# A decoder trunk on eight cores: one channel group instead of two follows the token tiles, the second becomes a plain slot with the last tiles between, the norm row comes in four row strips, and one P buffer set remains

## The chip, the cores and the metric

The kernel runs on all 8 cores of one Trainium2 chip, which are two dies of four cores each. The time of an execution is the time of the slowest core in microseconds (us) on the device. A kernel's time is the median of several executions.

Some executions fall in a slower state: one die shows a lower granted clock than the other (0.81 to 0.98 on the one, 0.98 to 0.99 on the other) and the time is 1.6% to 17.7% above the fastest of the same kernel in the same rounds. Those executions are marked slow; they are not compared with anything. All profiles that are read below are of fast executions. TensorE's clock has two levels in these traces, a granted share of 1.00 and one of 0.50; "full rate" and "half rate" below mean these two.

A core's trace is read against a set of marks (start of the first projection, start of the first full convolution, and so on), and where I say "median of the cores" I mean that I read the mark on each of the eight cores of one profiled execution and took the median.

## The reference, cut to what matters

One layer of a hybrid decoder trunk, run on a batch of prompts and on a batch of short samples:

```python
def layer(x, ...):
    m = mixer(rms_norm(x, g_mix_pre), ...)
    x = x + rms_norm(m, g_mix_post)
    f = conv_ffn(rms_norm(x, g_ffn_pre), ...)      # up-projection, conv(3), gelu gate, down-projection
    return x + rms_norm(f, g_ffn_post)

def mixer(xn, ...):
    a_val, a_gate, b_x, b_gate = split(xn @ w_in)
    u  = a_val * sigmoid(a_gate)                    # group A: 8 channel groups of 128
    ca = silu(layer_norm(causal_dwconv(u, 31 taps)))
    xc = causal_dwconv(b_x, 4 taps)                 # group B: 8 heads of 128
    h  = rglru(xc, ...)                             # a scan along the tokens
    cb = h * gelu(b_gate)
    return concat(ca, cb) @ w_out
```

Everything that the change touches lies in the first 410 us, in `rms_norm`, the projections with `w_in`, and the convolution of group A. Each core has 17 tiles of 128 tokens. A tile is loaded, squared and scaled by its norm, transposed on TensorE, and copied from PSUM (`ps` in the profiles, which the matmuls write) to SBUF (`sb_...`, which they read). The projections of this kernel read that copy and wait for it.

## The kernel before: the parts that the change and the argument touch

A tile is normed on ScalarE (square, logarithm, exponential) and VectorE (one multiply with the gain row), and turned on TensorE:

```python
def p0_norm(n):
    ...
    act(xs, xt, AF.Square, ..., accum=c[:, 0:1])           # ScalarE, reads the loaded tile
    act(c[:, 1:2], c[:, 0:1], AF.Ln, ...)
    act(c[:, 2:3], c[:, 1:2], AF.Exp, ...)
    stt(xs, xt, c[:, 2:3], T["grow0"], mult, mult, ...)    # VectorE, 2.35 us
    if n + XD(n) < 17: p0_load(n + XD(n))

def p0_turn(n):
    # 16 transposes of 128x128 into two PSUM banks (6 and 7),
    # then copies PSUM -> xna (and xnp) on VectorE and ScalarE
    ...
```

The first channel groups follow the tiles as they come. In the kernel before these are two groups (j = 0 and 1), so per pair of tiles TensorE has two gate and value projections and two pieces of convolution:

```python
load_w(4, after=[("xt0",)])                 # four 1 MB weights first
p0_load(1)
for n in range(2, 5):
    p0_load(n, [(f"wu{n - 1}",)])           # tile 2 waits for weight 1, and so on
...
for g in range(5):
    for j in range(2):
        if g > 0 and j == 0:
            p0_norm(2 * g + 2)
            p0_norm(2 * g + 3)
        ...
        early(g, j)                         # gate and value projection of this piece of tokens
        if g >= 2:
            early_conv(g - 2, [j])          # 31 taps as matmuls with diagonal matrices
        if g > 0:
            p0_turn(2 * g + 2 + j)
```

After the last tile, seven rounds of the same kind follow: gate and value projections of one channel group, the convolution of that group, and a P block of group B (its `b_x` projection, gates and scan). I call this the steady stretch. The P blocks work on the tokens in `xnp`. The next stage, the Q stage, runs group B over the tokens in `xna` (projections `X` and `b`, gelu, gates, scan) and the LayerNorm of group A. The turn into it reads:

```python
bx7 = triple(); P_bx(7, bx7)                # last P projection, into a group of three PSUM banks
...
QX, QB = 3, 0
proj(QX, "X", 0, ACT3)                      # next projection, into the same three banks
...
proj(QB, "b", 0, CAT3, g0=30)
P_gate(7, "wab"); P_sig(7, "p1", V_BA)      # sigmoid
bs = ln_sum("A3b", QX); act(T["mu"], ...)
P_gate(7, "wxb"); P_sig(7, "p3", V_BX)      # sigmoid
Q_gelu(0, QB); done_w("b", 0)               # gelu: a table load of 1.28 us ahead of it
bq = ln_sum("A3", QB)                       # TensorE, needs the banks QB that gelu reads
```

All buffers have fixed places in SBUF, from a table of offsets. A buffer may lie over another whose life has ended. The first write to it then waits for the last reader of the old one.

## Time and profile before

The median of three executions is 1850.44 us (1849.97 to 1850.83).

| | before |
|---|---|
| span of the slowest core in the profile | 1849.0 us |
| TensorE busy | 95% of it |
| first projection, median of the cores | 20.9 us |
| twelfth tile (n = 11 in the code) turned | 105.1 us |
| first full convolution starts | 140.6 us |
| last P projection ends | 373.1 us |
| second X projection starts (Q stage under way) | 404.7 us |
| up-projection starts | 702.0 us |

The first line of the page that I use is the busy table. It gives for each engine the busy time in us, its share of the span and the number of instructions:

```profile
PE 1764.0 (95%) x10470; PEld 918.3 (50%) x10470; DVE 989.7 (54%) x998; ACT 569.1 (31%) x1016; POOL 131.6 (7%) x248
```

PE is TensorE, DVE is VectorE and ACT is ScalarE. TensorE bounds the kernel. Which stretch of time could be saved does not stand in this line, so here are the windows of the same core (core 3). Each line is one stretch: its limits, its length, the busy time of each engine with its instruction count, the mean clock that TensorE was granted (1.00 is full rate, half rate counts as 0.50), and the share of the DMA engines in use with the GB/s:

```profile
20.00:40.00 20.00, 9.78 (x96) 8.74 (x96) 10.75 (x12) 8.35 (x16) 0.00 (x0) 0.80 1.02 287
40.00:60.00 20.00, 17.79 (x156) 14.63 (x157) 13.40 (x11) 14.68 (x27) 1.06 (x2) 0.86 0.79 256
60.00:80.00 20.00, 19.50 (x170) 15.01 (x169) 10.19 (x9) 9.14 (x17) 0.00 (x0) 1.00 0.54 144
80.00:100.00 20.00, 19.50 (x203) 17.54 (x201) 9.72 (x12) 10.67 (x20) 1.06 (x2) 1.00 0.27 52
100.00:120.00 20.00, 17.73 (x169) 12.78 (x167) 10.77 (x11) 9.35 (x17) 1.06 (x2) 1.00 1.03 243
120.00:140.00 20.00, 16.06 (x160) 12.12 (x158) 13.65 (x11) 10.42 (x14) 2.64 (x5) 0.86 0.72 129
```

TensorE is idle for 10.2 us from 20 to 40 us. It is almost full from 60 to 100 us at full rate, and it loses again from 100 to 140 us, partly at a reduced clock. The view of TensorE's waits (line, what it waited for, us in total, times, longest) for 20 to 410 us says which waits those are (four of its lines):

```profile
PE ps L473 <- DVE sb_xs_107 L372: 6.2, 1, 6.2
PE ps L473 <- DVE sb_xnp_138 L351: 6.2, 3, 3.9
PE ps L378 <- ACT sb_gbg_95 L345: 3.9, 1, 3.9
PE ps L378 <- ACT sb_bxpZ L343: 2.2, 1, 2.2
```

L473 is the transpose, L378 the matmul. The 6.2 us are the wait for tile 2, which was loaded late behind a weight. The 3.9 us to `sb_xnp` lie at the last tiles. The wait for `sb_gbg` is the late gelu, and the wait for `sb_bxpZ` is the evacuation of the last P projection: these two are the turn. The timeline of TensorE around 77 us shows the loop at its best. The columns are start, length, engine, line, operation, number of instructions, and in brackets the idle time ahead with what ended it:

```profile
74.20 1.03 PE L378 MATMUL ps<-sb_xna_137,sb_wu_192 128*128 128x256 bf16 x8 [0.50 <-DVE sb_xna_137 L351]
...
90.43 1.03 PE L378 MATMUL ps<-sb_xna_137,sb_wu_192 128*128 128x256 bf16 x8 [0.50 <-DVE sb_xna_137 L351]
```

The same projection (the first weight of a piece) comes back after 90.43 - 74.20 = 16.2 us, with only 0.5 us of idle time ahead. So a pair of tiles costs 16.2 us here, and matmul work fills it.

### The profile page before, as it was taken

The numbers are of one execution on the slowest core, as the hardware profiler recorded it, in microseconds if no ns is written. First come the engines' busy times: TensorE is split into PE (matmuls) and PEld (weight loads), VectorE is DVE, ScalarE is ACT, GpSimd is POOL, SyncE is SP. The second block draws the span as 40 slices with busy tenths as digits, with TensorE's granted clock in tenths as the row PEclk, the third lists the DMA queues.
The fourth block names the chain that finished last, engine by engine and source line by source line (L and its number), as shares of the span: only waits on it lengthen the run. The fifth ranks groups of instructions, "written<-read, shape, count | busy, mean of one in ns | idle before, by whom it ended". The sixth has DMA issues, their size and how long they took to land.

```text
span 1849.0 us, 33818 instructions; the slowest of 8 cores (1840.2 to 1849.0 us)
## 1 busy us (share of the span) xinstructions
PE 1764.0 (95%) x10470; PEld 918.3 (50%) x10470; DVE 989.7 (54%) x998; ACT 569.1 (31%) x1016; POOL 131.6 (7%) x248
## 2 busy tenths in 40 slices
PE   5989999989987999999999999999999999999996
PEld 3765555644443444555555544444555555544442
DVE  4564565458885564666666640001666666663245
ACT  4552442358882443222222211111222212211111
POOL 0010000001120001000000000001000000000000
PEclk8999999999998999999999999999999999999998
DMA  9482243212268438644333335556444433359556
GB/s 248 127 182 38 47 84 53 37 35 49 44 115 221 166 137 182 115 69 69 66 67 66 68 68 120 120 120 120 70 69 70 69 66 67 67 136 250 103 159 217
DMA packets 55318, 193.22 MB, mean 104 GB/s; under 512 B 7393, under 2 KB 11361, under 8 KB 48993
## 3 DMA queue, kind: packets, MB, share of 16 engines
q0 software_dynamic: 30144, 110.34, 34.8%
q1 hardware_dynamic: 24994, 80.71, 13.0%
q8 instruction: 84, 1.38, 0.3%
q14 instruction: 96, 0.79, 0.2%
HBM read 266.52 MB, written 32.35 MB: 162 GB/s over the span
## 4 chain that ended last, share of the span: by engine, by line
PE 91%; DMA 3%; ACT 3%; issue 2%; DVE 1%; DVEq 0%; POOL 0%; ACTq 0%; SPq 0%; POOLq 0%
PE ps L378 90%; DMA sb_wo_213<-w_out 1%; PE ps L473 1%; DMA sb_wu_193<-w_in 1%; DMA sb_xt_106<-xall 1%; ACT L345 0%; PE ps L1159 0%; DMA sb_xt_96<-xall 0%; DVE sb_ht L372 0%; ACT sb_xs_1_132 L347 0%; ACT sb_t_1_128 L345 0%; ACT sb_t_0_114 L345 0%; DVE sb_xna_137 L351 0%; DVE sb_xs_102 L372 0%; DVE sb_xs_107 L372 0%
## 5 line engine op out<-in xcount | busy, mean ns | idle before, releaser
L351 DVE COPY sb_ve_120<-ps 128x1026 f32<-128x1026 f32 (+1 forms) x48 | 36.4, 801 | 297.4 <-PE ps L378 294.9
L351 DVE COPY sb_ve_134<-ps 128x1026 f32<-128x1026 f32 (+1 forms) x48 | 36.4, 801 | 114.0 <-PE ps L378 114.0
L372 DVE SCALAR_TENSOR_TENSOR sb_og_135<-sb_ge_133,sb_vecs,sb_og_135 128x1184 f32<-128x1184 f32 x48 | 69.7, 1452 | 5.7 <-DVE sb_og_135 L372 0.9
L372 DVE SCALAR_TENSOR_TENSOR sb_ov_136<-sb_ve_134,sb_vecs,sb_ov_136 128x1184 f32<-128x1184 f32 x48 | 69.7, 1452 | 5.0
L372 DVE SCALAR_TENSOR_TENSOR sb_ov_122<-sb_ve_120,sb_vecs,sb_ov_122 128x1184 f32<-128x1184 f32 x48 | 69.7, 1451 | 5.0
L372 DVE SCALAR_TENSOR_TENSOR sb_og_121<-sb_ge_119,sb_vecs,sb_og_121 128x1184 f32<-128x1184 f32 x48 | 69.7, 1451 | 5.0
L343 ACT COPY sb_dstg<-ps 128x512 f32<-128x512 f32 x36 | 20.9, 587 | 159.5 <-PE ps L378 159.5
L378 PE MATMUL ps<-sb_ubf_124,sb_diag_123 128*128 128x342 bf16 (+3 forms) x527 | 63.9, 284 | 1.2 <-DVE sb_ubf_124 L363 1.2
L378 PE MATMUL ps<-sb_ubf_110,sb_diag_109 128*128 128x342 bf16 (+3 forms) x527 | 62.3, 279 | 0.7 <-ACT sb_ca_199 L345 0.7
L343 ACT COPY sb_ffo<-sb_ve_134 128x32 f32<-128x32 f32 x24 | 5.3, 219 | 182.1 <-DVE sb_ve_134 L351 182.1
L343 ACT COPY sb_ffo<-sb_ve_120 128x32 f32<-128x32 f32 x24 | 5.3, 219 | 175.5 <-DVE sb_ve_120 L351 175.5
L345 ACT ACT_TABLE_LOAD x38 | 48.8, 1283 | 31.6 <-PE ps L378 19.6
L378 PEld LDWEIGHTS ps<-sb_ubf_124,sb_diag_123 128*128 128x128 bf16 x527 | 46.6, 100 | 18.4 <-issue 1.6
L345 ACT ACTIVATE sb_og_135<-sb_og_135 128x1184 f32<-128x1184 f32 x24 | 28.6, 1191 | 84.0 <-DVE sb_og_135 L372 84.0
L378 PEld LDWEIGHTS ps<-sb_ubf_110,sb_diag_109 128*128 128x128 bf16 x527 | 44.9, 97 | 17.6 <-issue 0.9
L345 ACT ACTIVATE sb_og_121<-sb_og_121 128x1184 f32<-128x1184 f32 x24 | 28.6, 1190 | 79.6 <-DVE sb_og_121 L372 79.6
L343 ACT COPY sb_ge_119<-ps 128x1026 f32<-128x1026 f32 (+1 forms) x48 | 31.4, 707 | 32.9 <-PE ps L378 32.9
L343 ACT COPY sb_ge_133<-ps 128x1026 f32<-128x1026 f32 (+1 forms) x48 | 31.4, 706 | 27.4 <-PE ps L378 27.4
L378 PE MATMUL ps<-sb_xn_139,sb_wp_214 128*128 128x512 bf16 (+1 forms) x192 | 35.2, 325 | 0.5 <-DVE sb_xn_139 L351 0.5
L378 PE MATMUL ps<-sb_xn_139,sb_wp_216 128*128 128x512 bf16 (+1 forms) x192 | 35.1, 325 | 0.3 <-ACT sb_ge_119 L343 0.3
L378 PE MATMUL ps<-sb_xn_142,sb_wp_214 128*128 128x512 bf16 (+1 forms) x192 | 35.1, 325 | 0.1
L378 PE MATMUL ps<-sb_xn_139,sb_wp_225 128*128 128x512 bf16 (+1 forms) x192 | 35.2, 325 | 0.0
(736 smaller groups left out, 4084.9 us busy)
## 6 DMA issues: line engine op xcount, KB each, us to landing
f_scr<-sb_dstg SPq DMA_DIRECT2D x36, 256.0 KB, 3.5
sb_xt_96<-xall SPq DMA_DIRECT2D x5, 1024.0 KB, 11.0
sb_x_0_117<-xall SPq DMA_DIRECT2D x5, 1024.0 KB, 5.0
h_scr<-sb_x_0_117 SPq DMA_DIRECT2D x5, 1024.0 KB, 5.4
sb_xt_101<-xall SPq DMA_DIRECT2D x4, 1024.0 KB, 12.3
sb_xt_106<-xall SPq DMA_DIRECT2D x4, 1024.0 KB, 11.0
sb_x_1_131<-xall SPq DMA_DIRECT2D x4, 1024.0 KB, 4.9
sb_wp_214<-w_up POOLq DMA_DIRECT2D x8, 512.0 KB, 6.2
```

Of the source, the lines that this page charges most:

```text
L343: S.op("act", lambda e: e.copy(out=out, in_=in_), reads, writes)
L345: S.op("act", lambda e: e.activation(out=out, in_=in_, func=func, scale=scale, bias=bias), reads, writes)
L351: S.op("dve", lambda e: e.tensor_copy(out, in_), reads, writes)
L372: S.op("dve", lambda e: e.scalar_tensor_tensor(out, a, s, b, op0, op1), reads, writes)
L378: S.op("pe", lambda e: e.matmul(out, lhsT, rhs, start=start, stop=stop, skip_group_check=skip), reads, writes)
L473: S.op("pe", lambda e, pb=pb, j=j, k=k: e.transpose(pb[:, 128 * j:128 * j + 128], xs[:, 128 * k:128 * k + 128], identb[:]), [ks, "identb"] ...
```

## The change

Its intent is to get through the tiles sooner. With one channel group following, a pair of tiles costs TensorE less, two weights are enough to start with, and the last tiles are turned between the thirds of the second group's projections, where TensorE has other work. The norm row is loaded in four pieces to partitions 0, 32, 64 and 96, so that four small matmuls with one row each can spread it. The Y set of P buffers goes, and the loop over the groups becomes uniform. At the turn, the counter of the PSUM bank groups skips one (`trip["n"] += 1`), so that the next projection does not need the banks that are still being evacuated, and gelu runs ahead of the two sigmoids. All buffers get new places.

The core of the diff (cut: the table of places, lifetimes, `vecs` loaded ahead of tile 0, the building of the conv diagonals in two parts, and the rewritten inner order of the steady stretch):

```diff
-        seq += [("g", 0), ("v", 0), ("g", 1), ("v", 1), ("g", 2), ("v", 2), ("x", 0), ("x", 1), ("g", 3), ("v", 3), ("x", 2)]
-        for j in range(4, 8):
+        seq += [("g", 0), ("v", 0), ("g", 1), ("v", 1), ("x", 0)]
+        for j in range(2, 8):
 ...
-        load("sp", r_su, T["grow0"][0:1, :], grows_d[0:1, :], [], ...)
+        for c in range(4):
+            load("act", r_ga, T["grow0"][32 * c:32 * c + 1, 512 * c:512 * c + 512], grows_d[0:1, 512 * c:512 * c + 512], [], ...)
 ...
-        load_w(4, after=[("xt0",)])
+        load_w(2, after=[("xt0",)])
         p0_load(1)
         for n in range(2, 5):
-            p0_load(n, [(f"wu{n - 1}",)])
+            p0_load(n, [("wu0",)])
 ...
-        for g in range(5):
-            for j in range(2):
-                ... early(g, j); early_conv(g - 2, [j]); p0_turn(2 * g + 2 + j)
+        for g in range(1, 5):
+            early(g)
+            p0_turn(2 * g + 2)
+            p0_norm(2 * g + 4)
+            if g >= 2:
+                early_conv(g - 2)
+            p0_turn(2 * g + 3)
+            p0_norm(2 * g + 5)
 ...
+        p0_turn(12); p0_norm(14)
+        proj(bg, "g", 1, ACT3, only=0)
+        early_conv(3); done_w("v", 0)
+        p0_turn(13); p0_norm(15)
+        proj(bg, "g", 1, ACT3, only=1)
+        ...
+            if j == 7:
+                trip["n"] += 1
 ...
         proj(QB, "b", 0, CAT3, g0=30)
+        Q_gelu(0, QB)
+        done_w("b", 0)
         P_gate(7, "wab")
-        P_sig(7, "p1", V_BA)
         bs = ln_sum("A3b", QX)
         ...
+        P_sig(7, "p1", V_BA)
+        bq = ln_sum("A3", QB)
         P_gate(7, "wxb")
         P_sig(7, "p3", V_BX)
-        Q_gelu(0, QB)
```

## The prediction

> **What bounds the kernel now.** By the page's busy table TensorE is busy 95% of 1849 us. The 20 us windows place its idle time: about 32 us before 200 us, 1.4 us from there to 370, some 29 us from 370 to 600, little later. The change keeps the matmul work, so only idle times and half-rate stretches can move.
>
> *Start.* In the waits and the timeline, TensorE waits 3.0, 3.5 and 4.9 us for the first two tiles and 6.2 us for tile 2, which landed only at 31.0 us: its load waits for the second of four 1 MB weights (20.1 us), then took 10.8 us. From 54 to 106 us TensorE has almost no gap: with two channel groups, 16.2 us of work per pair of tiles. From 106 to 144 us it loses 1.9, 3.9 and 0.7 us around the last tiles, plus half rate after: 16 transposes take 1.87 us instead of 1.06, 62 conv matmuls 5.26 instead of 3.64. [...]
>
> *Turn into the Q stage.* At 376.7 us TensorE waits 2.2 us for the evacuation of the last P block (same PSUM triple as the next projection), at 399 and 400 us 0.7 and 3.9 us (gelu queued behind two sigmoids and a 1.28 us table load). Two half-rate stretches add about 3.4 us.
>
> **What changes.**
> 1. Norm row in four row strips [...] instead of 7.2 us in series: worth 0.3 us, as the row's last copy ends at 11.0 us and the first norm could start at 10.8. Vecs ahead of tile 0 costs about 0.7.
> 2. Two weights instead of four ahead of tiles 2 to 4: tile 2 lands near 22 us.
> 3. Per pair of tiles TensorE has 9.2 us (3.5 gate and value, 2.1 transposes, 3.6 conv). But evacuation, square and norm (1.0+2.7 us ScalarE, 2.35 VectorE) stand between the two transposes, then a 1.3 us evacuation: about 11.5 us per pair. So the loop turns from matmul-bound to chain-bound, with gaps of 1 to 6 us. I expect the eleventh tile turned near 80 us instead of 106, with 27.4 us less work done: the early arrival is mostly given back.
> 4. The last tiles lie between the thirds of the second group's projections: one or two gaps of 2 us, no half rate. At the start of its conv (near 108 us; the old kernel reaches the same state at 144 less 31 us) about 4 us are gained.
> 5. One P buffer set: about 1.3 us lost at j=2, as much as the old gaps at 189 and 229 us. Neutral.
> 6. The skipped triple and the earlier gelu remove the 2.2 and most of the 4.6 us. But VectorE's chain into the Q stage does not move, and ScalarE is nearly full from 425 us: about 4.5 us.
>
> **Prediction.** 1850.4 - 4.3 - 4.5 = about 1841 us, 8 times in 10 within 1830 to 1851. Faster by over 2%: 0.01; within 2%: 0.97; slower: 0.02.
>
> **Signs.** Right: tile 2 lands by 24 us; TensorE's idle in 50 to 106 us rises to over 8 us, waiting for VectorE's copies of xna; no half-rate stretch in 106 to 144; no 2.2 and 3.9 us waits near 377 and 400; same length from 600 us on. Wrong: tile loads waited for after 40 us, or the loop at full rate.
>
> **What would make it wrong.** Half rate through the sparser loop; weights colliding with tiles 7 to 9; the new placement making a load of w_out or w_up wait; ScalarE in the Q stage eating the gain.

## The result, and the profile after

| | before | after |
|---|---|---|
| median | 1850.2 us of 4 | 1889.88 us of 4 |
| all executions | 1849.97, 1850.44, 1850.83, 1849.01 | 1848.32, 2089.98 (slow), 1846.8, 1931.45 (slow) |
| ratio of fast executions | | 0.9986 (95% interval 0.9962 to 1.0011) |

A ratio here is the mean time of one kernel's fast runs over that of the other's of the same rounds, so it is not quite the ratio of the medians quoted. Two of the four executions of the changed kernel fell in the slow state, and they pull its median to 1889.88 us, outside the predicted range. That says nothing of the change: in later rounds the kernel before also had such executions, for instance 2106.47 and 2139.37 us. The two fast executions lie inside the range. But the gain is 2 or 3 us, not the 9.4 us (1850.4 - 1841) that I had summed up. This section and the experiments are about where the rest went.

The busy table tells nothing of it:

```profile
PE 1765.4 (96%) x10375; PEld 910.2 (49%) x10375; DVE 988.6 (54%) x994; ACT 564.2 (31%) x1000; POOL 131.6 (7%) x248
```

It misleads here: the busy time hardly moved (1764.0 and 1765.4 us), since matmuls at half rate count as busy for longer (32 of them 6.51 instead of 3.65 us, below), while the time that TensorE spent at half rate moved a good deal, as the windows of the changed kernel (its slowest core, core 1) show:

```profile
20.00:40.00 20.00, 13.57 (x108) 11.43 (x106) 10.52 (x11) 12.04 (x20) 0.00 (x0) 0.74 0.99 334
40.00:60.00 20.00, 13.95 (x106) 10.15 (x104) 11.70 (x10) 12.25 (x22) 3.17 (x6) 0.74 0.83 238
60.00:80.00 20.00, 16.67 (x154) 13.73 (x152) 12.71 (x10) 11.70 (x23) 0.54 (x1) 0.91 0.84 156
80.00:100.00 20.00, 17.49 (x184) 12.94 (x183) 15.48 (x13) 11.30 (x17) 0.53 (x1) 0.91 0.89 217
100.00:120.00 20.00, 19.21 (x159) 12.39 (x158) 9.54 (x10) 9.58 (x14) 2.11 (x4) 1.00 0.42 68
120.00:140.00 20.00, 20.00 (x137) 11.87 (x136) 4.39 (x6) 3.53 (x4) 1.07 (x2) 1.00 0.15 25
```

From 20 to 40 us TensorE now does more, since tile 2 comes early. From 100 us on there is almost no idle time, as intended. But from 40 to 100 us it is idle for 20 us - 13.95, 16.67 and 17.49 us busy, so 11.9 us in all, and the granted clock is 0.74 and 0.91 where it was 0.86 and 1.00. The waits over 20 to 410 us are of another kind:

```profile
PE ps L377 <- DVE sb_xna L350: 5.9, 3, 2.5
PE ps L472 <- DVE sb_xs L371: 5.1, 2, 4.0
PE ps L472 <- DVE sb_xna L350: 4.7, 2, 2.4
PE ps L472 <- DVE sb_xnp L350: 2.5, 1, 2.5
PE ps L377 <- ACT sb_gbg L344: 2.5, 1, 2.5
```

The wait for tile 2 has shrunk from 6.2 to 4.0 us, and the 2.2 us at the turn are gone (L377 is now the matmul, L472 the transpose). In their place stand five waits of 2.3 to 2.5 us, each for VectorE's copy of a turned tile. Here are two of them on the timeline:

```profile
41.68 1.05 PE L472 MATMUL ps<-sb_identb,sb_xs 128*128 128x128 bf16 x16 [1.11 <-DVE sb_xs L371]
45.15 1.87 PE L472 MATMUL ps<-sb_identb,sb_xs 128*128 128x128 bf16 x16 [2.42 <-DVE sb_xna L350]
49.53 6.51 PE L377 MATMUL ps<-sb_xna,sb_wu 128*128 128x256 bf16 x32 [2.52 <-DVE sb_xna L350]
...
63.73 3.65 PE L377 MATMUL ps<-sb_xna,sb_wu 128*128 128x256 bf16 x32 [0.83 <-DVE sb_xna L350]
```

The second transpose and the projection at 49.53 us are not the same length as their like: 16 transposes take 1.87 instead of 1.05 us, 32 matmuls 6.51 instead of 3.65 us. The clock records of this core say half rate from 45.2 to 55.4 us, so nearly the whole 6.51 us ran at half rate.

To see where the few microseconds go, I split each core's span at the marks. Each entry gives the length of the stretch, TensorE's idle time in it, and what half rate cost in it (half of the busy time at granted clock 0.5, an estimate from the lengths above, 1.87 instead of 1.05 us and 6.51 instead of 3.65 us; the clock records begin only at 23 to 26 us, and I counted what lies before as half rate, since 16 transposes take 1.86 us there as they do at 0.5); medians of the eight cores, in us:

| stretch | before | after |
|---|---|---|
| to the first projection | 20.9: 10.0, 5.4 | 21.1: 10.8, 5.3 |
| tile stretch, to the first full convolution | 119.9: 19.2, 6.7 | 93.1: 19.2, 11.6 |
| steady stretch, to the end of the last P projection | 232.6: 1.4, 0 | 263.7: 1.3, 0 |
| turn, to the second X projection | 31.4: 6.7, 3.2 | 25.2: 2.5, 1.7 |
| Q stage, to the first output projection | 138.3: 13.8, 4.0 | 138.7: 14.6, 3.9 |
| output projection, to the up-projection | 157.9: 13.4, 8.8 | 159.4: 13.9, 9.3 |
| from there to the last matmul | 1125.7 | 1125.6 |

The changed kernel has one more convolution and gate and value pair left after the tiles, which is the 263.7 - 232.6 = 31.1 us of the steady stretch. So its tile stretch is to be read as 93.1 + 31.1 = 124.2 us, against 119.9 us: 4.3 us longer in this pair of profiles, where I had predicted 4.3 us less. The idle time is the same 19.2 us in both. What differs is half rate, 11.6 against 6.7 us. The turn gained 6.2 us. The end of the kernel is unchanged.

One pair of profiles is not enough for such a difference. Five profiles have the early code of the changed kernel (it, and the runs e1, e7, e9 and e10 below), and their last P projections end at 377.6, 375.3, 376.2, 376.3 and 377.2 us, on average 376.5. Two have the early code of the kernel before (it and e4): 373.1 and 376.5 us, on average 374.8. So the tile stretch lost about 1.7 us, between -1.2 and +4.5 us for single pairs. That is the measured size of what I predicted as -4.3 us: with two old profiles it is not clear of zero, but no pair comes near -4.3.

### The profile page after: what moved, and what is told of

Read it like the earlier page. It is cut to its first block, busy times and chain, and to the rows that moved or that the text cites. A ratio compares the mean times of both kernels' runs of the same rounds, so it can differ in the third digit from the quotient of the medians.

```text
span 1846.8 us, 33554 instructions; the slowest of 8 cores (1834.9 to 1846.8 us)
## 1 busy us (share of the span) xinstructions
PE 1765.4 (96%) x10375; PEld 910.2 (49%) x10375; DVE 988.6 (54%) x994; ACT 564.2 (31%) x1000; POOL 131.6 (7%) x248
## 4 chain that ended last, share of the span: by engine, by line
PE 91%; DMA 3%; ACT 3%; issue 2%; DVE 1%; DVEq 0%; POOL 0%; SPq 0%; ACTq 0%; POOLq 0%
PE ps L377 90%; DMA sb_wo<-w_out 1%; DMA sb_xt<-xall 1%; PE ps L472 1%; ACT sb_xs L346 1%; DMA sb_fl<-f_scr 0%; ACT sb_t L344 0%; PE ps L1127 0%; ACT L344 0%; DMA sb_wu<-w_in 0%; DVE sb_ht L371 0%; ACT sb_catA L344 0%; DVE sb_xna L350 0%; ACT sb_bxe L342 0%; ACT sb_tiny L344 0%
## 5 line engine op out<-in xcount | busy, mean ns | idle before, releaser
L377 PE MATMUL ps<-sb_xn,sb_wp 128*128 128x512 bf16 (+1 forms) x4608 | 750.9, 325 | 1.0 <-DVE sb_xn L350 0.5
L377 PEld LDWEIGHTS ps<-sb_xn,sb_wp 128*128 128x128 bf16 x4608 | 384.0, 97 | 367.7 <-issue 1.4
L377 PE MATMUL ps<-sb_wp,sb_hm 128*128 128x512 bf16 x1728 | 373.3, 379 | 0.0
L350 DVE COPY sb_ve<-ps 128x1026 f32<-128x1026 f32 x96 | 72.9, 801 | 411.7 <-PE ps L377 411.7
L377 PE MATMUL ps<-sb_xna,sb_wu 128*128 128x512 bf16 (+3 forms) x1600 | 273.8, 332 | 6.0 <-DVE sb_xna L350 5.9
L377 PEld LDWEIGHTS ps<-sb_wp,sb_hm 128*128 128x128 bf16 x1728 | 169.0, 98 | 203.4
L377 PEld LDWEIGHTS ps<-sb_xna,sb_wu 128*128 128x128 bf16 x1600 | 146.3, 101 | 131.8 <-issue 14.0
L371 DVE SCALAR_TENSOR_TENSOR sb_ov<-sb_ve,sb_vecs,sb_ov 128x1184 f32<-128x1184 f32 x96 | 139.3, 1452 | 10.7 <-DVE sb_ov L371 0.5
L371 DVE SCALAR_TENSOR_TENSOR sb_og<-sb_ge,sb_vecs,sb_og 128x1184 f32<-128x1184 f32 x96 | 139.4, 1452 | 10.0
L377 PE MATMUL ps<-sb_ubf,sb_diag 128*128 128x342 bf16 (+3 forms) x1023 | 124.0, 282 | 0.8 <-DVE sb_ubf L362 0.8
L377 PEld LDWEIGHTS ps<-sb_ubf,sb_diag 128*128 128x128 bf16 x1023 | 88.1, 97 | 36.9 <-issue 0.9
L377 PE MATMUL ps<-sb_wo,sb_catA 128*128 128x512 bf16 (+1 forms) x320 | 73.8, 398 | 7.9 <-DVE sb_ht L371 4.7
L377 PE MATMUL ps<-sb_wo,sb_catB 128*128 128x512 bf16 (+1 forms) x320 | 73.3, 395 | 6.4 <-DMA sb_wo<-w_out 6.4
L342 ACT COPY sb_dstg<-ps 128x512 f32<-128x512 f32 x36 | 20.9, 586 | 159.6 <-PE ps L377 159.6
L377 PE MATMUL ps<-sb_xnp,sb_wu 128*128 128x496 bf16 x256 | 54.9, 372 | 1.3 <-ACT sb_p L344 1.3
```

Source lines behind the costliest of these rows:

```text
L342: S.op("act", lambda e: e.copy(out=out, in_=in_), reads, writes)
L350: S.op("dve", lambda e: e.tensor_copy(out, in_), reads, writes)
L371: S.op("dve", lambda e: e.scalar_tensor_tensor(out, a, s, b, op0, op1), reads, writes)
L377: S.op("pe", lambda e: e.matmul(out, lhsT, rhs, start=start, stop=stop, skip_group_check=skip), reads, writes)
```

## The experiments

My theory had four parts. (A) The chain of norm, transposes and copies sets the pace of the new loop, as predicted, and the repeated 2.4 us waits make TensorE fall to half rate, which takes the gain away. (B) The early weights and tiles are worth something and are given back to (A). (C) The norm row is worth nothing. (D) The turn gains by gelu's place and by the skipped bank group. The rivals were: the idle time alone makes up the loss and the clock is only a bystander; the load order or the row is what lost; the new placement of buffers causes the difference; and the turn's gain has nothing to do with the two edits. Runs e1 to e4, e5 to e8 and e9 to e12 were each made on one chip, which differed between the three sets.

### e1: the changed kernel again

No edit.

> The change, unaltered, timed in more rounds beside the others. Median over the cores of the profiled run: first full-size conv matmul near 114 us, last P projection ends near 377.6 us (373.1 in the old kernel), projection X1 starts near 402.8 (404.7). Ratio to the old kernel 0.997 to 1.000. If the four runs of the first look misled, it would come out under 0.995 or over 1.001.

Measured: 1847.3 us against 1852.22 us for the kernel before on this chip, ratio of the fast runs 0.9973 (0.996 to 0.9985). The change is a gain of about 5 us on this chip, 0.27%. Its tile stretch was 91.4 us with 10.2 us lost to half rate.

### e2: useless matmuls in the waits

```diff
+        def fill(n):
+            b = stb["b"] % 6
+            for _ in range(n):
+                mm(PS[:, 512 * b:512 * b + 512], T["wu0"][:, 4, :], T["wu0"][:, 0:4, :]..., True, True, [("wu0",)], PK(b))
         early(0)
+        fill(8)
         p0_norm(3)
         p0_turn(2)
+        fill(6)
         p0_turn(3)
+        ... fill(3), fill(8) in group 1, then fill after the second turned tile of each group
```

The added matmuls write a PSUM bank that the next projection starts anew, so results are right. They shorten no chain. They keep TensorE busy, and they do one thing more: they read the buffer of the first weight (`wu0`), so the next load into it cannot start before they end. The two weight loads that `done_w("v", 0)` releases are issued at 81.8 and 82.2 us (median of the cores) instead of 76.6 and 78.3 us in e1. That is not where the gain comes from: ScalarE waits for no tile load after 40 us in the changed kernel either (0.9 us on one core).

> The change plus useless 512-column matmuls in the waits of TensorE in the tile loop, so that its clock stays at full rate; nothing else moves. Half-rate theory: the projections of groups 2 and 4 of the loop take 3.7 us each instead of 6.5 and 5.3, the conv of the second channel group starts 4 to 6 us earlier (about 108 to 110 us instead of 114), the last P projection ends at about 372 to 374, and the run is 2 to 5 us faster than the change. Rival, chain theory: ScalarE and VectorE set the pace of the loop whatever TensorE's clock is, so the conv starts within 1.5 us of 114 and the time stays.

Measured: 1844.28 us, 0.9951 (0.9936 to 0.9966), about 4 us less than e1 on the same chip. The twelfth tile is turned at 79.5 us and the full convolution starts at 107.0 us (83.0 and 111.7 in e1). Half rate in the tile stretch costs 2.9 instead of 10.2 us. TensorE's timeline, on core 0:

```profile
49.20 3.65 PE L377 MATMUL ps<-sb_xna,sb_wu 128*128 128x256 bf16 x32 [1.82 <-DVE sb_xna L350]
...
60.55 3.65 PE L377 MATMUL ps<-sb_xna,sb_wu 128*128 128x256 bf16 x32 [0.40 <-DVE sb_xna L350]
...
71.89 3.65 PE L377 MATMUL ps<-sb_xna,sb_wu 128*128 128x256 bf16 x32 [0.78 <-DVE sb_xna L350]
```

The projections take 3.65 us each time, where one took 6.51 us. They begin at 49.20, 60.55 and 71.89 us: 11.35 us per pair of tiles at full rate, still waiting for the copies. That is the chain, and the marks 79.5 and 107.0 us are those of my prediction (80 and 108 us). So the chain was right, and half rate is what kept the changed kernel from it. Adding work that nobody needs made the kernel faster, and no account in which the clock is a bystander allows that. It also closes the sum: with 2.9 us of half rate the last P projection ends at 370.7 us, 5.8 us before the unfilled average (376.5) and 4.1 us before the old one (374.8), about the 4.3 us that I had predicted.

### e3: VectorE's multiply behind the second tile's copies

```diff
             p0_turn(2 * g + 2)
-            p0_norm(2 * g + 4)
+            p0_norm(2 * g + 4, 1)          # ScalarE's part
             if g >= 2:
                 early_conv(g - 2)
             p0_turn(2 * g + 3)
+            p0_norm(2 * g + 4, 2)          # VectorE's multiply, 2.35 us
             p0_norm(2 * g + 5)
```

> The change, with VectorE's half of one norm of each pair (the multiplication by the row) moved behind the second transposed tile's evacuation; ScalarE's half stays. Chain theory: that multiplication (2.35 us) stands between the two transposes of a pair, so a pair of tiles takes about 10 us instead of 11.3 to 14, TensorE's 2.5 us waits at the head of each group fall under 1.3 us, the half-rate stretches go with them, the conv starts at about 107 to 110 us instead of 114, and the run is 3 to 6 us faster than the change. Half-rate theory alone, with the waits untouched by order: no more than 1 us. If tile loads bound the loop, nothing changes either.

Measured: 1849.27 us, but with two slow executions in six; 0.9976 (0.9962 to 0.999) for the fast ones, no gain over e1 (0.9973). The pace did become what I expected. From the timeline of TensorE on core 2:

```profile
59.11 3.65 PE L377 MATMUL ps<-sb_xna,sb_wu 128*128 128x256 bf16 x32 [0.50 <-DVE sb_xna L350]
...
68.45 3.65 PE L377 MATMUL ps<-sb_xna,sb_wu 128*128 128x256 bf16 x32 [0.50 <-DVE sb_xna L350]
...
80.64 1.87 PE L475 MATMUL ps<-sb_identb,sb_xs 128*128 128x128 bf16 x16 [3.35 <-DVE sb_xs L371]
```

9.34 us per pair, which is the matmul work. But at 80.64 us the next tile is not there, and TensorE waits 3.35 us and falls to half rate (1.87 us for 16 transposes). ScalarE shows why in its own timeline on the same core:

```profile
83.40 1.91 ACT L346 ACTIVATE sb_xs<-sb_xt 128x2048 bf16<-128x2048 f32 x1 [6.44 <-DMA sb_xt<-xall]
```

It waits 6.44 us for the load of one of the last tiles, and 3.85 us for the next (two such waits on every core, 6.4 to 10.3 us together). The loads of tiles 13 and 14 are issued at 70.7 and 72.9 us here (median of the cores), and two weight loads at 70.3 and 72.0 us, beside them. In the changed kernel the weights come at 77.6 and 80.0 us, after the loads of tiles 13 and 14 (73.8 and 77.2 us). So a faster loop ran into its loads, and the gain was given back as a new wait; that the weights in between are what delays the tiles fits these times, but no run tests it (see e12). The full convolution starts at 109.5 us, 2.2 us before e1's, where the pace alone would have given more.

### e4: the old structure with the turn alone

```diff
             done_w("x", i)
+            if j == 7:
+                trip["n"] += 1
 ...
         proj(QB, "b", 0, CAT3, g0=30)
+        Q_gelu(0, QB)
+        done_w("b", 0)
         P_gate(7, "wab")
-        P_sig(7, "p1", V_BA)
         ...
```

> The old kernel with only two late parts of the change: the skipped PSUM triple before the last conv and the gelu ahead of the gates. If the change lost in the tile phase and gained in the turn to the Q stage: the last P projection ends at 373 as in the old kernel, X1 starts about 5 to 6 us earlier than 404.7, and the run is 3 to 5 us faster than the old kernel, faster than the whole change. If the later ScalarE-bound stage eats the gain: under 2 us.

Measured: 1848.37 us, 0.9975 (0.9963 to 0.9988). This equals the whole change (0.9973 on the same chip). So a dozen moved lines at the turn are worth as much as everything together, and the rest of the change nets to nothing that these intervals show. The turn went from 31.4 to 25.1 us, 6.3 us less. But 3.1 us came back in the Q stage, 141.4 instead of 138.3 us. ScalarE on core 3 shows a wait there:

```profile
421.76 1.28 ACT L345 ACT_TABLE_LOAD   x1 [1.28 <-DVE sb_bxpZ L627]
```

The table load ahead of the first tanh waits for VectorE's scan of the last P block (L627). In the old table of places the first tanh buffer lies over that block's `p1Z`. This suggested that the new placement matters after all, and e7 tests it.

### e5: four weights first again

```diff
-        load_w(2, after=[("xt0",)])
+        load_w(4, after=[("xt0",)])
         p0_load(1)
         for n in range(2, 5):
-            p0_load(n, [("wu0",)])
+            p0_load(n, [(f"wu{n - 1}",)])
 ...
-        load_w(4, after=[("xt0",)])
```

> The change with the old order of loads: four weights ahead of tiles 2 to 4 instead of two. Theory (the tile loop is paced by its own chain and clock, but it can only start when tile 2 is there): tile 2 lands near 31 us instead of 24, the conv of the second group starts 5 to 7 us later than the change's 112 to 114, the last P projection ends near 382. Rival (early arrival is worthless, the loop waits anyway): within 1.5 us of the change.

Measured: 1852.97 us, 1.002 (1.0006 to 1.0034). The last P projection ends at 383.3 us, against 375.3 to 377.6 us in the five profiles with the changed kernel's early code. On core 3 TensorE's waits show one of 12.2 us for a normed tile. So the load order is worth about 6 to 8 us in the new structure. It did what I had said, and the rival that it had cost something is out.

### e6: one row instead of four

```diff
-        for c in range(4):
-            load("act", r_ga, T["grow0"][32 * c:32 * c + 1, ...], ...)
+        load("sp", r_su, T["grow0"][0:1, :], grows_d[0:1, :], ...)
 ...
-            mm(PS[:, 512 * c:512 * c + 512], ones[32 * c:32 * c + 1, :], T["grow0"][32 * c:32 * c + 1, ...], ...)
+            mm(PS[:, 512 * c:512 * c + 512], ones[0:1, :], T["grow0"][0:1, ...], ...)
```

> The change with the norm row undone: one row load ahead of everything on its queue, one strip, matmuls one after the other. Theory: the row is off the path, because TensorE's first projection waits for tile 1 and then for tile 2; first projection at 20.5 to 21.5 us as in the change (21.0), conv start within 1 us. Rival (the strips are worth their design): everything 2 to 3 us later.

Measured: 1845.96 us, 0.9983 (0.9968 to 0.9997). The first projection starts at 20.4 us, not later than with the strips (20.7 to 21.1 us in the others of the changed structure with strips and no fillers). The strips bring nothing, and TensorE's timeline says why. First the kernel before, then the changed one:

```profile
3.05 7.16 PE L378 MATMUL ps<-sb_grow_51,sb_ones 1*128 1x512 f32 x8 [3.05 <-DMA sb_grow_51<-grows]
```

```profile
2.77 3.74 PE L377 MATMUL ps<-sb_grow,sb_ones 1*128 1x512 f32 x4 [2.77 <-DMA sb_grow<-grows]
6.78 2.04 PE L377 MATMUL ps<-sb_grow,sb_ones 1*128 1x512 f32 x2 [0.26 <-DMA sb_grow<-grows]
9.51 2.04 PE L377 MATMUL ps<-sb_grow,sb_ones 1*128 1x512 f32 x2 [0.69 <-DMA sb_grow<-grows]
```

Each piece needs two matmuls. On this core the four pieces landed one after another, so that the last matmuls could only start at 9.51 us. In the kernel before, all eight were done by 3.05 + 7.16 = 10.2 us. Where two pieces landed close together, their strips did run in parallel, as on core 3 of e1:

```profile
9.94 2.20 PE L377 MATMUL ps<-sb_grow,sb_ones 1*128 1x512 f32 x4 [3.44 <-DMA sb_grow<-grows]
```

Four matmuls of two pieces take 2.20 us here, while two of one piece take 2.04 us above. But the last piece still ends at 12.1 us, later than the single row. So the strips do what they were meant to, and it is the four loads, landing apart, that give the gain away.

### e7: the old overlap of two buffers in the changed kernel

```diff
-    "t1_0": 12320, "t3_0": 101728,
+    "t1_0": 101728, "t3_0": 12320,
```

With this, the first tanh buffer of the Q stage lies over `p1Z` of the last P block again. Nothing else changes.

> The change with the places of two equally large Q buffers exchanged, so that the first tanh writes over the P block 7 buffer and must wait for its scan, as in the old kernel. Placement theory (why the two turn changes keep only half their gain in the old kernel): the stretch from X1 to the output projection grows from 138.8 to about 141 us, ScalarE shows a 1.3 us wait for VectorE's scan before the first tanh. Rival (the different gain has another cause): it stays within 0.5 us of 138.8.

Measured: 1850.44 us, 1.0007 (0.9991 to 1.0023), so the gain of the whole change is gone (the change itself was not run on this chip, but e6, with the change's places, stands at 0.9983 there). The Q stage takes 141.5 us instead of 138.7. On core 0 ScalarE waits ahead of the table load; below it, in a fence of its own, is the changed kernel's same core, where it does not:

```profile
421.29 1.28 ACT L344 ACT_TABLE_LOAD   x1 [1.53 <-DVE sb_hP L350]
```

```profile
421.00 1.28 ACT L344 ACT_TABLE_LOAD   x1
```

So two entries in the table of places are worth about 3 us. In the diff they are two among all the places that moved, and nothing marks them.

### e8: split, fillers, and a later weight load

```diff
+        (e3's split of p0_norm)
+        (e2's fill, now with an optional bank)
         early(0)
+        fill(10)
         p0_norm(3)
         p0_turn(2)
+        fill(8)
         p0_turn(3)
 ...
         conv_diag(1)
+        fill(12)                            # ahead of tile 12, where e3 waited
         p0_turn(12)
         ...
         early_conv(3)
-        done_w("v", 0)                      # releases two weight loads
+        fill(3, 1)
         p0_turn(13)
         ...
         A_val(1, bv)
+        done_w("v", 0)
         done_w("v", 1)
```

> Candidate: the change with the moved multiplication, useless matmuls in the waits that this leaves (after group 0, between tiles 2 and 3, 4 and 5, before tiles 12 and 13), and the loads of the next two weights issued after tile 16 instead of before tile 13. If chain, clock and late loads together are what was lost: a pair takes 9.4 us, no ScalarE wait over 3 us for tiles 14 and 15, conv start at 102 to 105 us (107 with useless matmuls alone, 109.5 with the move alone, 112 to 114 in the change), last P projection ends at 366 to 369, ratio to the old kernel 0.993. If a new wait takes their place, the conv starts at 106 or later.

Measured: 1837.7 us, 0.9937 (0.9924 to 0.995). It is the best kernel (e12, below, cannot be told from it) and beats both. The twelfth tile is turned at 74.1 us, the last P projection ends at 367.2 us, and half rate costs 2.4 us in the tile stretch. ScalarE's waits for tile loads are down to one per core, of 1.5 to 3.1 us. The two weight loads are issued at 86.7 and 87.2 us (median of the cores), well after those of tiles 13 and 14 (68.2 and 70.3 us). Split, fillers and later weights give more together (about 9 us at the end of the last P projection, 376.5 to 367.2) than alone (e2 370.7, e3 373.2).

### e9 and e10: the two halves of the turn, each taken away

```diff
 (e9)        done_w("x", i)
-            if j == 7:
-                trip["n"] += 1
 (e10)    proj(QB, "b", 0, CAT3, g0=30)
-        Q_gelu(0, QB)
-        done_w("b", 0)
         P_gate(7, "wab")
+        P_sig(7, "p1", V_BA)
         ...
         P_sig(7, "p3", V_BX)
+        Q_gelu(0, QB)
+        done_w("b", 0)
```

> The change without the skipped PSUM triple. Theory (the skip is worth the 2.2 us wait before X0 and the half-rate stretch it starts): the turn, from the last P projection's end to X1, grows from 25.2 to 27 to 29 us, with a wait of about 2.2 us for the evacuation of the last P block. Rival (VectorE's chain into the Q stage hides the skip, as it does not move): under 1 us.

> The change with the old order of gelu and gates. Theory: the turn grows from 25.2 to 28 to 29 us, with waits of 3.9 us for the gelu and 0.7 for a sigmoid in place of 2.5 for the gelu. If skip and gelu hide each other's gain, the two runs together do not sum to 6.2 us.

Measured: e9 1850.4 us, 0.9989 (0.9975 to 1.0002); e10 1850.01 us, 0.9984 (0.997 to 0.9997). The intervals overlap each other and those of the changed kernel, so the verdict must come from the length of the turn:

| | gelu late | gelu early |
|---|---|---|
| without skip | 31.4 us (before) | 25.4 us (e9) |
| with skip | 29.8 us (e10) | 25.2 us (after) |

Gelu's place gives nearly all. The skip gives 1.6 us alone and 0.2 us on top. TensorE's waits from 365 to 412 us on core 0 of e9 show that the wait which the skip removes is back, and that it costs nearly nothing:

```profile
PE ps L377 <- ACT sb_bxpZ L342: 2.2, 1, 2.2
PE ps L377 <- ACT sb_p1Z L344: 1.3, 1, 1.3
PE ps L377 <- ACT sb_gbg L344: 0.3, 1, 0.3
```

The 2.2 us at the evacuation are there in full, and the wait for gelu has shrunk from 2.5 us (after) to 0.3 us. TensorE comes 2.2 us later to a point where it had to wait anyway. The turn takes 24.9 to 25.4 us in every run with the early gelu, whether half rate costs 1.7 us in it (after) or nothing (e4, e8, e9): with gelu early, its length is not set by TensorE's own work. I had expected e9 to lose about what the skip removes; that was wrong. In e10 the gelu wait is 3.8 us again on that core, and the stage after is 1.4 us shorter (137.3 against 138.7 us), so of the 4.6 us that it loses at the turn a third comes back.

### e11: the old structure with all that helped

```diff
-    "t1_0": 53440, "t2_0": 31232,
+    "t1_0": 31232, "t2_0": 53440,
+        (the turn, as in e4)
             if g == 0:
+                fill(16)
                 p0_turn(2)
+                fill(9)
                 p0_turn(3)
+        ... fillers also between the last tiles
```

If the fillers alone were the lesson, the old structure should gain as much from them.

> The old kernel with the two turn changes, with the places of two Q buffers exchanged so that the first tanh waits for no scan, and with useless matmuls in its own waits (before tiles 2, 3, 14 and 16). Question: is it worth anything that only one group follows the tiles, once the clock is kept? If the structure is worth little: conv of the third group starts at 134 to 137 us (140.6 in the old kernel; the best candidate's 103.5 plus 31.2 is 134.7), turn 25, X1 to output projection 138.8, ratio about 0.994, equal to the best candidate. If one following group is better in itself: 138 or later and a ratio over 0.996. If worse: under 133.

Measured: 1845.59 us, 0.9961 (0.9947 to 0.9974). The Q stage is 139.0 us, so the mended placement returned the 3 us of e4. But the full convolution starts at 142.7 us, where I expected 134 to 137, and the last P projection ends at 375.3 us, no earlier than the average of the old early code (374.8 us). Half rate did fall, from 7.7 us (e4) to 3.7 us. Counting fillers as busy, idle time fell from 20.2 to 12.5 us, but the fillers did not bring the marks forward. Its chain of loads still waits: 4.3 us for a constant from setup and 1.0 us for a weight on core 3. Why nothing more came of the clock here I have not settled. What the run does give is a comparison: with turn, placement and clock mended in both, the new structure (e8) ends its last P projection at 367.2 us and the old one at 375.3 us. This is the second branch of the expectation (138 or later, ratio over 0.996). But e8 also has the split, which e11 lacks. With fillers alone the new structure (e2) ends at 370.7 us, 4.6 us before e11, and the ratios of these two, 0.9951 and 0.9961, cannot be told apart.

### e12: e8 with the call for the two weights at its old place

```diff
         early_conv(3)
+        fill(3, 1)
         done_w("v", 0)                      # stays where the change has it
```

> The best candidate with the two weight loads where the change has them, before tile 13. If these loads delay tiles 14 and 15: ScalarE waits over 3 us for a tile near 80 us and the conv starts 1.5 to 4 us later than the candidate's 103.5. If they don't: within 1 us.

Measured: 1842.18 us, 0.9943 (0.9928 to 0.9959), with the last P projection at 367.5 us against 367.2 us in e8. That looks like the second branch, weights that do no harm. But the edit moved the call and not the loads. The fillers read the buffer of the first weight, so the load into it waits for them (on core 2 of e12 the one ahead of tile 13 ends at 87.8 us). GpSimd, which issues the weights, shows it on core 2, in e3 and then in e12:

```profile
70.90 0.53 POOL L380 DMA_DIRECT2D sb_wu<-w_in  x1 [16.37 <-PE ps L377]
72.64 0.53 POOL L380 DMA_DIRECT2D sb_wu<-w_in  x1 [1.21 <-PE ps L475]
```

```profile
88.31 1.07 POOL L380 DMA_DIRECT2D sb_wu<-w_in  x2 [34.16 <-PE ps L377]
```

The median of the cores in e12 is 86.7 and 87.2 us, the same as in e8. So e12 is in effect a second run of e8 on another chip, and whether e8 needs the later loads is untested. That the waits for tiles fell from 6.4 to 10.3 us (e3) to at most 3.4 us (e8 and e12), with the weights out of their way in both, speaks for it but does not show it.

## Why the prediction was right or wrong, point by point

The median fell outside the range because two of four executions were slow. Its fast executions lie inside, close to the upper end, and that is partly luck: two misses of opposite sign partly cancel. What failed is the sum: -4.3 for the tiles, -4.5 for the turn. The tiles gave about +1.7 us, the turn -6.2.

**Tile stretch: the failed step is items 3 and 4.** I wrote "I expect the eleventh tile turned near 80 us instead of 106" and "near 108 us" for the start of the convolution. Both came 3 to 6 us late (84.7 and 113.9 us; 83.0 and 111.7 us in e1). (Its "eleventh" counts from 0; it is the twelfth tile of the tables.) The mechanism of item 3 was right. The loop is bound by a chain, I had worked out 11.5 us per pair and e2 measured 11.35 us, and e2 reached 79.5 and 107.0 us. What I had left out of the sum is the term that I named only as a risk, "half rate through the sparser loop". It cost 9.9 to 11.6 us in the tile stretch of the five profiles with the changed early code (10.6 on average), where the old early code loses 6.7 and 7.7 us (7.2 on average). The difference is 3.4 us, and the sum had none of the 10.6 us in it, since item 4 promised "no half rate" and item 3 left it out. With most of it removed (e2) the predicted 4 us appear. The idle time is 19.2 us in both first profiles. So the early tiles did remove the large waits, the chain filled in small ones of the same sum, and these cost clock as well (half rate takes 11.6 us of the tile stretch, against 6.7 us before).

I misjudged this because I took it that only longer idle times cost the clock. That was an estimate of mine, and no trace had shown it. The loop's waits are 2.3 to 2.5 us each (the 4.0 us for tile 2 come before the loop), and half rate follows several of them. In the traces of the first two profiles (before and after) every stretch of one rate lasts a whole multiple of 3.41 us (336 clock records on 16 cores, without the last of each core, which the end of the profile cuts). On core 1 of the changed kernel half rate lasts 28.1 to 38.3, 45.2 to 55.4, 75.9 to 79.3 and 89.5 to 93.0 us, so 3, 3, 1 and 1 times 3.41 us. I call the pieces of 3.41 us between these limits windows. Cut at these limits, the windows view of that core reads:

```profile
41.78:45.20 3.42, 1.00 (x17) 0.86 (x16) 3.22 (x3) 3.23 (x5) 0.00 (x0) 1.00 0.76 249
45.20:48.60 3.40, 1.81 (x16) 1.55 (x16) 2.17 (x1) 3.09 (x7) 0.00 (x0) 0.50 0.84 277
48.60:52.00 3.40, 2.47 (x12) 1.75 (x13) 3.40 (x4) 0.20 (x1) 0.00 (x0) 0.50 0.90 207
52.00:55.40 3.40, 3.40 (x18) 2.35 (x16) 0.24 (x1) 1.22 (x3) 3.08 (x6) 0.50 0.90 280
...
72.50:75.90 3.40, 0.90 (x10) 0.78 (x9) 3.40 (x4) 2.04 (x4) 0.00 (x0) 1.00 0.23 31
75.90:79.30 3.40, 3.40 (x18) 2.43 (x17) 1.88 (x1) 1.12 (x3) 0.54 (x1) 0.50 0.85 306
```

A window in which TensorE was busy for 1.00 us of 3.42 is followed by half rate, and so is one with 0.90 us. A window at half rate with 1.81 or 2.47 us busy is followed by another at half rate, and one with 3.40 us ends it. I counted all such windows up to 1700 us in the traces, on all eight cores of the fourteen profiles:

```
TensorE's busy share of a window     windows    followed by half rate
at full rate,  under 40%                 977      973
at full rate,  40% to 50%                214       41
at full rate,  50% and over      about 52200        0
at half rate,  under 70%                 530      530
at half rate,  70% to 80%                 99       55
at half rate,  80% and over              970        0
```

A recount on the first two profiles alone gives, in the same order, 155 of 155, 5 of 24 and 0 of 7391 at full rate, and 88 of 88, 12 of 14 and 0 of 158 at half rate. The ends of the matmuls in a trace are modelled, so the shares are approximate. In these runs, then, half rate went with the busy share of a window and not with the length of a single gap: a full-rate window with under 40% busy, so more than 2.05 us idle, was followed by half rate 973 of 977 times, and after a half-rate window with 80% or more busy the full rate came back all 970 times. Where a wait falls matters too. On core 1 of the changed kernel the wait of 2.50 us up to 75.07 us lies within one window (72.5 to 75.9 us, 0.90 us busy), and half rate follows. On core 5 the same wait of 2.50 us, up to 71.90 us, falls into two (67.92 to 71.33 and 71.33 to 74.74 us, 1.47 and 2.84 us busy), and the clock stays at 1.00. That may be why the cores of one execution differ (in e3 the full convolution starts between 105.8 and 112.2 us, depending on the core); I have argued this and not shown it. That the lost clock costs the time is shown, by e2 (half rate 2.9 instead of 10.2 us, convolution at 107.0 instead of 111.7 us).

**Start (items 1 and 2).** Item 2 was right: tile 2 is used at 24.3 us, and e5 shows that the order of the loads is worth 6 to 8 us. Item 1 was right that the strips are worth next to nothing, but not why: I took it that they make the row earlier and that this is hidden. They do run in parallel when their pieces are there (four matmuls of two pieces in 2.20 us, core 3 of e1, where two of one piece take 2.04 us), but the four pieces landed apart, so the row was not there earlier (e6).

**Last tiles (item 4).** Right in kind. From 106 to 144 us TensorE is now busy 37.2 of 38 us at full clock (core 1), where it was 31.1 us (core 3 before). But this gain is inside the tile stretch's sum and was spent before.

**One P buffer set (item 5).** Right: neutral. The steady stretch has 1.3 us of idle time, as against 1.4 us.

**Turn (item 6).** The sign was right and the size was too small: 6.2 us instead of "about 4.5". I had held that VectorE's chain would take some of it, and 0.4 us came back in the Q stage (138.3 to 138.7 us). I also gave the skip more than it deserves. Gelu's place is the gain (31.4 to 25.4 us), since gelu stood behind two sigmoids and a table load of 1.28 us. ScalarE's timeline after the change, on core 0, shows what a table switch costs:

```profile
395.78 1.41 ACT L344 ACTIVATE sb_xc<-sb_bxe,sb_vecs 128x1232 f32<-128x1232 f32 x1 [6.51 <-DVE sb_bxe L350]
397.21 1.28 ACT L344 ACT_TABLE_LOAD   x1
398.50 1.13 ACT L344 ACTIVATE sb_gbg<-ps 128x1154 f32<-128x1154 f32 x1
```

The load starts 0.02 us after the activation ahead of it ends, and the next activation starts 1.29 us after the load's start, so a switch costs 1.3 us here.

**Placement.** I had listed the new placement as a risk for the loads of `w_out` and `w_up`. It was an unplanned benefit at the tanh buffer, 3 us (e4, e7), without which the change would have gained nothing (1.0007).

**The signs that I had named.** Right: tile 2 by 24 us (24.3 us), no half rate from 106 to 144 us, no 2.2 us wait near 377 us, the same length in the up-projection (1125.7 and 1125.6 us), no wait for tile loads after 40 us (but for 0.9 us on one core). Half right: TensorE's idle time from 50 to 106 us rose from 1.5 to 5.8 us, not to over 8, since the matmuls between were slower. Wrong: "no 3.9 us wait near 400", where 2.5 us remain. And the sign that should have warned me is the clock: the granted clock from 50 to 106 us is 0.89, and it was 1.00.

**What stays open.** Why the old structure gained so little from fillers (e11). Whether the later weight loads are part of e8's gain, which e12 was to test and did not. And the output-projection stretch differs by up to 3.8 us between profiles (155.8 to 159.6 us) with waits for loads of `w_out`, which I could not tie to any edit.

## What to carry to other kernels

If a change thins out the work of TensorE, read the granted clock in the trace, and the busy share between the limits at which that clock changes, not only the idle time: here, with changes a multiple of 3.41 us apart, a handful of waits of 2.4 us cost about 3 us of clock on top of themselves, and useless matmuls in the waits won that back. Mend the chain and the clock together (e8 gained 9 us where the parts gave 3 to 6), and look at what the faster loop then waits for. Check in the trace that an edit did what it was to do: a filler that reads a buffer holds up the next load into it, and so e12 moved a call and not its loads. And run the parts of a large change one at a time: a dozen lines at one turn were worth as much as the whole, and two entries in a table of buffer places decided whether it gained at all.
